# Two more pairs by seven products in the dense groups of a hybrid encoder block, with some low parts made by adding transfers

## The chip, the core and the metric

The kernel runs on one core of one Trainium2 chip. The metric is the device time of one execution in microseconds (us). TensorE (PE) multiplies, VectorE (DVE) and ScalarE (ACT) work element by element, GpSimd (POOL) here mainly issues transfers, SyncE (SP) issues nearly all loads. Each engine runs its own list of instructions in order and waits on semaphores for the others.

## The reference, cut to what matters

One encoder layer, 256 rows wide in the sequence and 4096 in the model, float32 throughout:

```python
xn = rms_norm(x, norm_in_g)
q, k, v, z_a, a_c, g_c, z_c = split(xn @ w_in)          # 4096 x 14336
y_a = rms_norm(chunked_attention(q, k, v, rel_table), attn_out_g) * silu(z_a)
y_c = rms_norm(conv_module(a_c, g_c, ...), conv_out_g) * silu(z_c)
h = x + concat([y_a, y_c]) @ w_out                       # 4096 x 4096
gate = sigmoid(rms_norm(h, ple_norm_g) @ w_ple_gate + b_ple_gate)   # 4096 x 4096
h = h + gate * (p @ w_ple)
out = rms_norm(h, final_g)
```

Nearly all work is in the products of a 256 x 4096 activation with w_in, w_out and w_ple_gate.

## The kernel before, in words

**High and low parts.** Each float32 operand is split into a high part, rounded to the format fp32r that PE multiplies, and a low part, the difference. A product of two blocks is three matmuls: high by high (kind 0), low by high (kind 1), and high by low (kind 2), where the second factor is the weight. The weights are split as they arrive (`parts_of`, L199): ACT casts the tile `wt` into `wh`, DVE subtracts it from `wt` into `wl`. `wt` has five buffers, `wh` and `wl` three each.

**Groups and pairs.** A product is made in groups of 1024 output columns (two blocks j of 512, called apart) by 256 rows (two halves h of 128). The 4096 rows of a weight are 32 blocks of 128; two of them (k0, k1) are a *pair*, so a group walks over 16 pairs. `mixed_product` (L344) makes one group in the four PSUM banks `acc`, one 128 x 512 result each, and for each pair takes one of two ways:

- A *plain* pair is the eight block products of a 2 x 2 by 2 x 2 block multiplication, 8 x 3 = 24 matmuls of 128x512.
- A pair *by sevens* (marked `*` or `+`) uses a scheme in seven products, 21 matmuls. It needs sums of the four weight blocks w00, w01 (of k0) and w10, w11 (of k1): ua = (w00 + w01, w01 + w11), then ub0 = ua1 + w11 and ub1 = ub0 + w10, all on DVE (L469, L470, L476, L477), each pair of sums split again on ACT and DVE into `uh` and `ul`. It also needs four combinations s of the activation blocks, which are made once (`combine_again`, L287: one 512-wide sum, then `combined_parts`, L261: four 128-wide operations and the split) and kept in tiles. The products are called P1 to P7 and are multiplied in the order P1, P5, P7, P2, P3, P6, P4; P1, P5, P6, P7 gather in four helper banks, which are worked into the results once a group, after its last pair by sevens (`on_helpers`, `helper_sums` L511, into the tiles z). P2 and P3 use k1's weight blocks w10 and w11. Of the activation, block (k0, second half) is not read by the seven products.

An order is a text such as `dense` (L329), which names the pairs of a group in order, with their marks. `dense` has eight pairs by sevens, all even ones; `late` (L342) has four. The combinations of the even pairs stand in tiles of their own.

**The stages.** First come groups for the convolution, queries, keys and values, in other orders, with convolution taps as filling work on DVE; the mark `+` there has the sums ua made by a transfer from GpSimd that adds to what a first transfer wrote (L423). Then `w_pw` (two groups), then the *dense groups*: four gate groups z_a and z_c (`gated`, L1064), four groups of the output projection w_out (loop at L1134, the first in order `late`, while its operands are still being made), three of the last stage (`gated_pair`, L1171, the first in order `late`) and a last group in order `final`, written out by hand.

**What sets the order.** The framework's planner places instructions: the program's text gives priorities and dependencies, and the planner, with its own costs, decides the order on each engine, which is then fixed. `later` is a queue of small pieces of work (evacuations, gating); after each pair a group takes some from it (`fill`). Tiles come from pools with a fixed number of buffers for each tag; an instruction that needs a new tile waits until a buffer of that tag is released. In the dense groups the pool `lpool` has two buffers for each tag: "stage" (the two tiles z of a group), "u", "uh" and "ul", and three for "row" (bias rows, final_g rows, scratch for combinations).

Of the kernel before, what the change touches and what calls it, by code (L numbers as in the profile page):

```python
# [16 lines left out]
P = 128  # L17
NB = 512
# [7 lines left out]
def hybrid_block(  # L26
# [184 lines left out]

    recent = []
# [48 lines left out]
    def combined_parts(dst, at, s, a, a01, a11, g, then=lambda ins: None):  # L261
# [6 lines left out]
        then(nc.vector.tensor_tensor(s3, a00, a10, ALU.subtract))  # L268
# [18 lines left out]
    def combine_again(dst, at, t, i, rows, then=lambda ins: None):  # L287

        a, s = rows
        then(  # L290
            nc.vector.tensor_tensor(
                a.rearrange("q (i t) -> q i t", t=T), t[:, i : i + 2, 0, :].bitcast(F32),
                t[:, i : i + 2, 1, :].bitcast(F32), ALU.add,
            )
        )
        return combined_parts(dst, at, s, a[:, :T], a[:, T : T + P], a[:, T + P :], 1.0, then)
# [27 lines left out]
    def units(text):  # L324

        return [(int(u.rstrip("*+")), u[-1] if u[-1] in "*+" else "") for u in text.split()]


    dense = units("1 0* 3 2* 5 4* 6* 7 8* 9 10* 11 12* 14* 13 15")  # L329
# [12 lines left out]
    late = units("1 3 5 7 9 11 13 15 0* 2 4* 6 8* 10* 12 14")  # L342

    def mixed_product(  # L344
# [14 lines left out]
        for n, (_, seven) in enumerate(order[: len(order) - n_left]):  # L359
# [45 lines left out]

        sums = {}
# [23 lines left out]
        last_seven = max((n for n, (_, seven) in enumerate(order) if seven), default=None)  # L430
        for n, (pair, seven) in enumerate(order):
# [41 lines left out]
            w1h, w1l = parts_of(w1, 2)[0]  # L473
# [7 lines left out]
            def s_of(i):  # L481
                t, at = comb[pair] if isinstance(comb, dict) else (comb[pair // 4], pair % 4)
# [576 lines left out]
    for c in range(2, D // NB):  # L1059
        if c % 2 == 0:  # L1060
            comb_tile(xS, 1)
        combine_again(xS[c // 2], 2 * (c % 2), xT[c], 0, sum_rows())()

    def gated(ys, c0, col, r_y, order, ahead):  # L1064

        _, z = sum_tiles()

        def on_helpers(helper):
            nc.scalar.copy(z[0][0], helper["P1"])
# [64 lines left out]
    for c0 in range(0, D // NB, 2):  # L1134
# [8 lines left out]
        def on_helpers(helper):  # L1143
# [9 lines left out]
            w_out[0], c0 * NB, yT, yS, dense if c0 else late, on_helpers,  # L1153
# [17 lines left out]
    def gated_pair(c0, order, ahead):  # L1171

        _, z = sum_tiles()
        rows, fgs = [], []
# [4 lines left out]
        def on_helpers(helper):  # L1179
            stt(z[0][0], helper["P1"], r_h[:, :1], rows[0], ALU.mult, ALU.add)  # L1180
# [179 lines left out]
```

## Time and profile before

| | |
|---|---|
| Median of three runs | 2029.99 us (2028.84 to 2030.45) |
| Span of the profiled execution | 2027.3 us |
| Lies around the span, against the median | 2.7 us |
| Clock granted to TensorE | full in all stages before the last |
| Busy PE, DVE, ACT, POOL | 99%, 95%, 60%, 2% |
| DMA | 436.70 MB, 215 GB/s |

The span runs from the first instruction to the last of one profiled execution; the runs are timed whole. A window's row gives its length, then busy time and number of instructions of each engine. A row of the timeline gives start, duration, engine, line, operation, tiles written and read, and in brackets how long the engine had been idle and what ended the wait.

### The profile page before, as it was taken

The page shows a single profiled execution, that of the slowest core. Times are in us where ns is not written, and L with a number is a line of the kernel's source. Part 1 is how long each engine was busy: PE and PEld are TensorE (multiplying, and loading weights), DVE is VectorE, ACT ScalarE, POOL GpSimd, SP SyncE. Part 2 cuts the span into 40 slices and gives each one's busy share as a digit, 9 for nine tenths or more (in the row PEclk, how much of TensorE's full clock was granted, in tenths as well). Part 3 has the DMA queues.
Part 4 walks back from the last instruction along what each step waited for, and adds up shares of the span by engine and source line. Part 5 has one row for each costly group of instructions (what it writes and reads, how often), then busy time and mean ns, then how long its engine had stood idle before and what let it go on. Part 6 is the DMA issues. An engine that isn't in the chain of part 4 may idle for free.

```text
span 2027.3 us, 26222 instructions
## 1 busy us (share of the span) xinstructions
PE 2010.3 (99%) x9064; PEld 1652.2 (81%) x9064; DVE 1917.8 (95%) x2732; ACT 1222.7 (60%) x1591; POOL 46.9 (2%) x50
## 2 busy tenths in 40 slices
PE   9999999999999999999999999999999999999997
PEld 7888888878888888788888888888888888888876
DVE  7999999889999998888899999999999999999998
ACT  7655545665656556776556566676665666665555
POOL 0000000000000000000000000000000000000000
PEclk9999999999999999999999999999999999999999
DMA  8787878678669867556666666676666656666765
GB/s 293 222 237 236 253 219 249 177 227 256 192 198 268 251 202 239 157 176 213 192 210 204 206 203 214 210 239 209 203 210 199 208 191 204 207 219 205 233 206 181
DMA packets 171168, 436.70 MB, mean 215 GB/s; under 512 B 13966, under 2 KB 17182, under 8 KB 171034
## 3 DMA queue, kind: packets, MB, share of 16 engines
q1 hardware_dynamic: 161952, 417.93, 64.1%
q0 software_dynamic: 8432, 16.25, 4.7%
q8 instruction: 71, 1.16, 0.3%
q10 hardware_dynamic: 650, 0.84, 0.1%
q14 instruction: 63, 0.52, 0.1%
HBM read 430.77 MB, written 4.19 MB: 215 GB/s over the span
## 4 chain that ended last, share of the span: by engine, by line
PE 92%; DVE 4%; issue 2%; DMA 1%; ACT 1%; POOLq 0%; POOL 0%; ACTq 0%; DVEq 0%
PE acc L387 71%; PE acc_P L387 17%; DVE wl L205 1%; PE tmp_ps L170 1%; DVE cv L726 1%; PE acc L229 1%; DMA wt<-in_w_in_dram 1%; DVE ul L205 1%; PE tmp_ps L898 0%; PE tmp_ps L882 0%; PE tmp_ps L916 0%; DVE cv L807 0%; PE tmp_ps L921 0%; ACT uh L204 0%; PE acc L375 0%
## 5 line engine op out<-in xcount | busy, mean ns | idle before, releaser
L387 PE MATMUL acc<-wh,big_t 128*128 128x512 f32 x4112 | 1271.6, 391 | 0.9 <-DVE y_c L1051 0.7
L204 ACT CAST wh<-wt 128x1024 fp32r<-128x1024 f32 (+1 forms) x737 | 708.8, 972 | 514.6 <-PE acc L387 359.8
L387 PEld LDWEIGHTS acc<-wh,big_t 128*128 128x128 f32 x4112 | 768.9, 188 | 160.4 <-DVE y_c L1051 1.1
L205 DVE TENSOR_TENSOR wl<-wt,wh 128x1024 fp32r<-128x1024 f32 (+1 forms) x737 | 816.7, 1120 | 33.4 <-ACT wh L204 27.8
L387 PE MATMUL acc<-wl,big_t 128*128 128x512 f32 x2056 | 794.5, 392 | 0.1
L387 PEld LDWEIGHTS acc<-wl,big_t 128*128 128x128 f32 x2056 | 385.5, 188 | 81.6 <-DVE wl L205 2.0
L204 ACT CAST uh<-ua 128x1024 fp32r<-128x1024 f32 x180 | 189.4, 1052 | 95.9 <-DVE ua L470 46.4
L205 DVE TENSOR_TENSOR ul<-ua,uh 128x1024 fp32r<-128x1024 f32 x180 | 219.5, 1220 | 5.0 <-ACT uh L204 3.2
L726 DVE SCALAR_TENSOR_TENSOR cv<-uT,dw,cv 128x255 f32<-128x255 f32 (+23 forms) x480 | 204.2, 465 | 1.1
L387 PE MATMUL acc_P<-uh,big_t 128*128 128x512 f32 x528 | 161.8, 391 | 0.1
L204 ACT CAST uh<-ub 128x1024 fp32r<-128x1024 f32 x92 | 96.8, 1052 | 92.5 <-DVE ub L477 81.1
L205 DVE TENSOR_TENSOR ul<-ub,uh 128x1024 fp32r<-128x1024 f32 x92 | 112.2, 1220 | 6.3 <-ACT uh L204 5.5
L387 PEld LDWEIGHTS acc_P<-uh,big_t 128*128 128x128 f32 x528 | 98.0, 188 | 23.0 <-ACT uh L204 3.5
L387 PE MATMUL acc_P<-ul,big_t 128*128 128x512 f32 x264 | 101.1, 391 | 0.1
L469 DVE TENSOR_TENSOR ua<-wt 128x512 f32<-128x512 f32 x105 | 72.0, 686 | 17.6 <-DMA wt<-in_w_in_dram 11.5
L387 PE MATMUL acc<-uh,big_t 128*128 128x512 f32 x272 | 84.1, 390 | 0.0
L387 PE MATMUL acc_P<-wh,big_t 128*128 128x512 f32 x272 | 84.0, 389 | 0.0
L470 DVE TENSOR_TENSOR ua<-wt 128x512 f32<-128x512 f32 x105 | 71.8, 684 | 3.2 <-DMA wt<-in_w_in_dram 3.1
L387 PE MATMUL acc_P<-uh,comb_t 128*128 128x512 f32 x228 | 70.2, 391 | 0.4 <-ACT uh L204 0.3
L477 DVE TENSOR_TENSOR ub<-ub,wt 128x512 f32<-128x512 f32 x92 | 63.1, 686 | 0.8
L476 DVE TENSOR_TENSOR ub<-ua,wt 128x512 f32<-128x512 f32 x92 | 62.9, 684 | 0.3
L387 PEld LDWEIGHTS acc<-uh,big_t 128*128 128x128 f32 x272 | 51.1, 188 | 10.6
(244 smaller groups left out, 1518.9 us busy)
## 6 DMA issues: line engine op xcount, KB each, us to landing
wt<-in_w_in_dram SPq DMA_DIRECT2D x416, 512.0 KB, 4.6
wt<-in_w_out_dram SPq DMA_DIRECT2D x128, 512.0 KB, 4.2
wt<-in_w_ple_gate_dram SPq DMA_DIRECT2D x128, 512.0 KB, 4.2
wt<-in_w_pw_dram SPq DMA_DIRECT2D x32, 512.0 KB, 4.7
ua<-in_w_in_dram SPq DMA_DIRECT2D x31, 512.0 KB, 4.5
ua<-in_w_in_dram POOLq DMA_DIRECT2D x31, 512.0 KB, 8.4
wt<-in_w_in_dram SPq DMA_DIRECT2D x31, 256.0 KB, 2.9
hc<-in_x_dram SPq DMA_DIRECT2D x8, 512.0 KB, 4.2
```

The lines of the kernel that those rows point to most:

```text
L170: nc.tensor.transpose(pt[:, i * T + h * P : i * T + (h + 1) * P], src[:, h, b] if len(src.shape) == 4 else src[:, h, b * P : (b + 1) * P], ...
L204: nc.scalar.copy(wh[:, :kc, :], wt[:, :kc, :]),
L205: nc.vector.tensor_tensor(wl[:, :kc, :], wt[:, :kc, :], wh[:, :kc, :].bitcast(F32), ALU.subtract),
L229: nc.tensor.matmul(acc, a, b[:, k, :], start=kb == 0 and kind == 0, stop=kb == kblocks - 1 and kind == 2,)
L387: nc.tensor.matmul(banks[name], a, b, start=name not in begun, stop=final and ends[name] == n and kind == 2 and not (left and name in "P2 ...
L469: plus(ua[:, 0], w0[:, 0], w0[:, 1])
L470: plus(ua[:, 1], w0[:, 1], w1[:, 1])
L476: plus(ub[:, 0], ua[:, 0], w1[:, 1])
L477: plus(ub[:, 1], ub[:, 0], w1[:, 0])
L726: nc.vector.scalar_tensor_tensor(cv[:, i, PAD - k :], uT[:, i, : T + k - PAD], dw[:, b, k : k + 1], cv[:, i, PAD - k :], ALU.mult, ALU.add,)
```

## The change

- The orders of the dense groups. `denser`, for the four gate groups and the second to fourth of the output projection, has ten pairs by sevens (the even ones, 13 and 9). `dense`, now only for the second and third group of the last stage, has nine (the even ones and 13). The order of the pairs within a group changes too. `late` and `final` stay.
- The combinations of pairs 13 and 9 are written into blocks of the activation tiles that no later product reads: block (k0, second half) of pairs 0, 2, 4, 6 for pair 13, and of pairs 8, 10, 12, 14 for pair 9. This is done once before the gates (both), once after the first group of the output projection (both), once after the first group of the last stage (13 only).
- A mark `-` in an order: five pairs of a `denser` group (2, 4, 8, 10 by sevens, 5 plain), four of a `dense` group (3, 5, 7, 9, all plain). There the low part of the weight's second block (k1) is not subtracted on DVE. ACT writes the negative of the weight, rounded, into a tile "low" (tag "stage"), and a transfer from GpSimd reads the same weights from memory again and adds them to it. The matmuls of kind 2 that use it are put off to the end of the next pair.
- Since "low" shares its tag with the tiles z, these are now allocated when the helpers are worked in, not at the group's start.

```diff
+    def high_and_minus(wt):
+        wh = wpool.tile([P, KC, NB], F32R, tag="wh", name="wh", bufs=3)
+        nc.scalar.copy(wh, wt)
+        low = spool.tile([P, KC, NB], F32R, tag="stage", name="low")
+        nc.scalar.activation(low, wt, AF.Identity, scale=-1.0)
+        return wh, low
...
         def split():
+            if at_places:
+                for i, (hi, lo) in enumerate(at_places):
+                    src = s[:, i * P : (i + 1) * P]
+                    nc.scalar.copy(hi, src)
+                    nc.vector.tensor_tensor(lo, src, hi.bitcast(F32), ALU.subtract)
+                return
...
-    dense = units("1 0* 3 2* 5 4* 6* 7 8* 9 10* 11 12* 14* 13 15")
+    dense = units("1 0* 2* 3- 4* 13* 5- 6* 8* 7- 10* 12* 9- 14* 11 15")
+    denser = units("1 0* 2*- 3 4*- 13* 5- 6* 8*- 7 10*- 12* 9* 14* 11 15")
...
+    def spare_places(tiles):
+        return [[t[:, 0, q, P:] for q in range(2)] for t in tiles]
+    places = {}
+    def combine_into_places(pair, tiles, first=0):
+        rows = sum_rows()
+        places[pair] = spare_places(tiles[first : first + 4])
+        t, i = tiles[pair // 2], pair % 2 * 2
+        combine_again(None, None, t, i, rows, at_places=places[pair])()
...
+        waiting = []
+        def add_waiting(n):
+            while waiting and waiting[0][0] <= n:
+                waiting.pop(0)[1]()
...
             if not seven:
-                for k in range(2):
-                    add_plain(n, k, *parts_of(wts[k], 2)[0])
+                add_plain(n, 0, *parts_of(wts[0], 2)[0])
+                if by_dma:
+                    wh, low = high_and_minus(wts[1])
+                    nc.gpsimd.dma_start(
+                        low, two_columns(w, 2 * pair + 1, col, apart), accum_op=ALU.add
+                    )
+                    add_plain(n, 1, wh, low, kinds=range(2))
+                    waiting.append((n + 1, partial(add_plain, n, 1, wh, low, kinds=(2,))))
+                else:
+                    add_plain(n, 1, *parts_of(wts[1], 2)[0])
+                add_waiting(n)
...
-            w1h, w1l = parts_of(w1, 2)[0]
+            if by_dma:
+                w1h, w1l = high_and_minus(w1)
+                nc.gpsimd.dma_start(
+                    w1l, two_columns(w, 2 * pair + 1, col, apart), accum_op=ALU.add
+                )
+            else:
+                w1h, w1l = parts_of(w1, 2)[0]
...
             def s_of(i):
+                if pair in places:
+                    return places[pair][i]
...
-            add("P2", block(k1, 0), (w1h[:, 0], w1l[:, 0]), n, True)
-            add("P3", s_of(3), (w1h[:, 1], w1l[:, 1]), n, True)
+            for name, x, j in (("P2", block(k1, 0), 0), ("P3", s_of(3), 1)):
+                part = partial(add, name, x, (w1h[:, j], w1l[:, j]), n, True)
+                part(kinds=range(2 if by_dma else 3))
+                if by_dma:
+                    waiting.append((n + 1, partial(part, kinds=(2,))))
...
+            add_waiting(n)
...
+    combine_into_places(13, xT)
+    combine_into_places(9, xT, 4)
...
-                ys, c0, o_z, r_y, dense,
+                ys, c0, o_z, r_y, denser,
...
-            w_out[0], c0 * NB, yT, yS, dense if c0 else late, on_helpers,
+            w_out[0], c0 * NB, yT, yS, denser if c0 else late, on_helpers,
...
+        if c0 == 0:
+            combine_into_places(13, yT)
+            combine_into_places(9, yT, 4)
...
+        if c0 == 0:
+            combine_into_places(13, hT)
```

More of the change, by code (lines that the diff above doesn't have):

```diff
@@ L259, in sum_rows, with combined_parts @@
         return [spool.tile([P, NB], F32, tag="row", name="comb", bufs=3) for _ in range(2)]
-    def combined_parts(dst, at, s, a, a01, a11, g, then=lambda ins: None):
+    def combined_parts(dst, at, s, a, a01, a11, g, then=lambda ins: None, at_places=None):
         a00, a10 = a[:, :P], a[:, P:]
@@ L285, in combine, with combine_again @@
         combined_parts(dst, at, s, a[:, :T], pts[1][:, :P], pts[1][:, P:], g[:, 1:2])()
-    def combine_again(dst, at, t, i, rows, then=lambda ins: None):
+    def combine_again(dst, at, t, i, rows, then=lambda ins: None, at_places=None):
         a, s = rows
@@ L295, in combine_again @@
         )
-        return combined_parts(dst, at, s, a[:, :T], a[:, T : T + P], a[:, T + P :], 1.0, then)
+        return combined_parts(
+            dst, at, s, a[:, :T], a[:, T : T + P], a[:, T + P :], 1.0, then, at_places
+        )
     def comb_tile(combs, n_kept=0):
@@ L324, in units @@
     def units(text):
-        return [(int(u.rstrip("*+")), u[-1] if u[-1] in "*+" else "") for u in text.split()]
-    dense = units("1 0* 3 2* 5 4* 6* 7 8* 9 10* 11 12* 14* 13 15")
+        return [
+            (int(u.rstrip("*+-")), "".join(f for f in "*+" if f in u), "-" in u)
+            for u in text.split()
+        ]
+    dense = units("1 0* 2* 3- 4* 13* 5- 6* 8* 7- 10* 12* 9- 14* 11 15")
+    denser = units("1 0* 2*- 3 4*- 13* 5- 6* 8*- 7 10*- 12* 9* 14* 11 15")
     first = units("0 1 3 5 7 9 11 13 15 2* 8 4* 10 6* 12 14")
@@ L358, in mixed_product @@
         n_left = len(left) // 2
-        for n, (_, seven) in enumerate(order[: len(order) - n_left]):
+        for n, (_, seven, _) in enumerate(order[: len(order) - n_left]):
             for name in ("P1", "P5", "P6", "P7", "P2", "P3", "P4") if seven else ("P2", "P3", "P4", "X"):
@@ L429, in mixed_product @@
                 after.enter_context(tc.issue_after(ins.ins))
-        last_seven = max((n for n, (_, seven) in enumerate(order) if seven), default=None)
-        for n, (pair, seven) in enumerate(order):
+        last_seven = max((n for n, (_, seven, _) in enumerate(order) if seven), default=None)
+        for n, (pair, seven, by_dma) in enumerate(order):
             if n < done:
@@ L1171, in gated_pair @@
     def gated_pair(c0, order, ahead):
-        _, z = sum_tiles()
-        rows, fgs = [], []
+        z, rows, fgs = [], [], []
         def on_begin():
@@ L1179, in on_helpers @@
         def on_helpers(helper):
+            z.extend(sum_tiles()[1])
             stt(z[0][0], helper["P1"], r_h[:, :1], rows[0], ALU.mult, ALU.add)
```

4 lines of the change are left out of this document (3 added, 1 removed).

## The prediction, made before the result was known

> **What bounds the kernel now.** I read the page first, then the chain of waits in order of time, then busy time by stretch, cut where the evacuation of each group of products begins.
>
> ```profile
> span 2027.3 us, 26222 instructions
> ...
> PE 2010.3 (99%) x9064; PEld 1652.2 (81%) x9064; DVE 1917.8 (95%) x2732; ACT 1222.7 (60%) x1591; POOL 46.9 (2%) x50
> ...
> PE 92%; DVE 4%; issue 2%; DMA 1%; ACT 1%; POOLq 0%; POOL 0%; ACTq 0%; DVEq 0%
> ...
> 1138.99 11.56 PE acc L387 x51
> ```
>
> The last row gives the price of one 128x512 matmul: 11.56 / 51 = 0.2267 us. The mean of 391 ns in other views is the latency of overlapping ones. TensorE sets the end, but VectorE is only 4 points behind, so the question is asked per group:
>
> ```profile
> 940.70:984.80 44.10, 44.10 (x195) 36.35 (x195) 35.75 (x56) 25.14 (x33) 0.00 (x0) 1.00 0.60 190
> ...
> 984.80:1067.90 83.10, 82.43 (x364) 67.89 (x363) 77.04 (x93) 50.58 (x59) 0.69 (x1) 1.00 0.64 203
> 1067.90:1149.70 81.80, 81.58 (x360) 67.25 (x359) 78.14 (x93) 49.15 (x54) 0.00 (x0) 1.00 0.64 205
> 1149.70:1231.10 81.40, 81.38 (x359) 67.10 (x358) 78.25 (x94) 49.02 (x54) 0.00 (x0) 1.00 0.65 207
> 1231.10:1314.00 82.90, 82.90 (x375) 68.88 (x375) 78.20 (x98) 50.33 (x61) 0.00 (x0) 1.00 0.66 214
> 1314.00:1404.40 90.40, 90.40 (x422) 74.78 (x422) 87.41 (x140) 59.24 (x85) 0.00 (x0) 1.00 0.68 223
> 1404.40:1485.60 81.20, 81.20 (x360) 67.21 (x359) 78.00 (x93) 48.53 (x57) 0.00 (x0) 1.00 0.63 207
> 1485.60:1567.70 82.10, 81.99 (x362) 67.58 (x361) 78.26 (x94) 48.94 (x59) 0.00 (x0) 1.00 0.63 205
> 1567.70:1651.20 83.50, 83.50 (x378) 69.34 (x377) 80.19 (x101) 52.12 (x67) 0.00 (x0) 1.00 0.64 208
> 1651.20:1741.50 90.30, 90.30 (x425) 75.18 (x424) 85.03 (x136) 59.12 (x91) 0.69 (x1) 1.00 0.62 197
> 1741.50:1829.10 87.60, 87.55 (x384) 71.35 (x383) 86.95 (x107) 53.48 (x64) 0.00 (x0) 1.00 0.66 212
> 1829.10:1917.20 88.10, 88.10 (x386) 71.76 (x385) 87.24 (x107) 52.40 (x64) 0.00 (x0) 1.00 0.67 216
> ```
>
> After the length come PE, PEld, DVE, ACT and POOL, then clock, DMA share and GB/s. The changed groups are rows 2 to 5 (gates), 7 to 9 (output projection) and 11 and 12 (last stage). A dense group is 360 matmuls, 360 x 0.2267 = 81.6 us: PE runs at its pace. But DVE is busy 78 of it, and 87 in the last stage. That leaves some 3.5 us a group before DVE becomes the bound.
>
> **The change, part by part.**
>
> *Matmuls.* A plain pair is 8 block products of 3 matmuls, a pair by sevens 7 of 3. Two more sevens in seven groups and one more in two: (7 x 2 + 2) x 3 = 48 matmuls fewer, 10.9 us if nothing else moved: 1.36 in each of the seven groups, 0.68 in the two.
>
> *VectorE.* Its prices are from start to start, since neighbours overlap:
>
> ```profile
> 1144.92 1.05 ACT L204 CAST wh<-wt 128x1024 fp32r<-128x1024 f32 x1 [1.67 <-PE acc L387]
> 1145.53 0.69 DVE L470 TENSOR_TENSOR ua<-wt 128x512 f32<-128x512 f32 x1 [0.33 <-DMA wt<-in_w_in_dram]
> 1146.14 0.68 DVE L476 TENSOR_TENSOR ub<-ua,wt 128x512 f32<-128x512 f32 x1
> 1146.86 0.69 DVE L477 TENSOR_TENSOR ub<-ub,wt 128x512 f32<-128x512 f32 x1
> 1147.46 1.22 DVE L205 TENSOR_TENSOR wl<-wt,wh 128x1024 fp32r<-128x1024 f32 x1
> 1148.60 1.22 DVE L205 TENSOR_TENSOR ul<-ua,uh 128x1024 fp32r<-128x1024 f32 x1
> 1149.73 2.48 DVE L1075 TENSOR_TENSOR z<-acc,z 128x512 f32<-128x512 f32 x4
> ...
> 1153.26 1.41 DVE L184 SCALAR_TENSOR_TENSOR qT<-qT,r_a,z 128x512 f32<-128x512 f32 x2
> 1153.44 1.04 ACT L204 CAST wh<-wt 128x1024 fp32r<-128x1024 f32 x1
> ```
>
> A 512-wide operation is 0.60 (0.72 between the two for ub, the second of which needs the first), a 1024-wide one 1.14. A plain pair is two low parts, 2.28. A pair by sevens is one 512-wide low part, four sums and three 1024-wide low parts: 0.60 + 0.60 + 0.60 + 0.72 + 0.60 + 3 x 1.14 = 6.54. So a pair moved costs DVE 4.26, and a low part made by a transfer gives back 1.14. The seven groups: 2 x 4.26 - 5 x 1.14 = +2.82. The last stage: 4.26 - 4 x 1.14 = -0.30. DVE then needs 78.14 + 2.82 = 80.96 in the second gate group, where PE needs 354 x 0.2267 = 80.25. **The bound changes engine**, and the saving is cut by the difference.
>
> *DVE's idle time.* No queue of dependent work runs quite without gaps. In the two last-stage groups, where DVE is nearly full now, it idles 87.60 - 86.95 = 0.65 and 88.10 - 87.24 = 0.86. The nearest rows on the other side:
>
> ```profile
> 183.10:268.60 85.50, 85.50 (x383) 70.80 (x382) 85.50 (x141) 44.25 (x49) 5.17 (x5) 1.00 0.81 240
> ...
> 445.90:531.70 85.80, 85.80 (x384) 71.00 (x383) 85.13 (x139) 47.01 (x53) 6.39 (x6) 1.00 0.89 254
> ```
>
> In the first DVE idles 0.00, but there convolution taps without a deadline fill each gap; dense groups have none. The upper bound is the 3.4 to 3.6 of today's gate groups. I take 0.75, by the rows nearest in kind and in load.
>
> *Combinations.* Five calls; each makes on DVE one 512-wide sum, four 128-wide operations and four 128-wide low parts, and four 128-wide copies on ACT.
>
> ```profile
> L291 DVE TENSOR_TENSOR comb<-big_t 128x512 f32<-128x512 f32 x16 | 11.0, 688 | 0.1
> ...
> L268 DVE TENSOR_TENSOR comb<-comb 128x128 f32<-128x128 f32 x31 | 8.9, 287 | 0.9 <-ACT comb L284 0.7
> ```
>
> With no overlap 0.69 + 8 x 0.287 = 2.99; with the 0.08 overlap of the rows above, 0.60 + 8 x 0.20 = 2.2; I take 2.6. The two for the gates (5.2) fall where DVE idles 44.10 - 35.75 = 8.35, mostly waiting for ACT: nothing, up to 5.2 if they are put off into the first gate group. The two of the output projection come after its first group, which has 90.40 - 87.41 - 0.75 = 2.24 to spare; 2.96 is left for the next one. The one of the last stage needs two "row" buffers of three, and two of these hold final_g until products put off into the next group are done, so its 2.6 falls there. DVE ends each first group on two plain pairs, with its buffers full, and part of the excess can be paid from that lead: between all and none, I take half, 1.48 and 1.30.
>
> *Low parts by transfer.* Each puts on ACT one more pass of about 1.05 (same size as the cast), and a pair by sevens casts three and a half tiles where a plain pair casts two, so ACT rises from 49 to 49 + 5 x 1.05 + 2 x 1.6 = 57.5 of 81, under PE. The negative may have to wait for one of the two "stage" buffers, and all later casts queue behind it on ACT, and DVE's low parts behind those. In the gates both hold the gate's sums until the products at L184: the first is free at 1153.26 + 1.41 = 1154.7, 5.4 us into a group that starts at 1149.3, and the first negative (pair 2, after pairs 1 and 0) is wanted some 8 us in, so no wait; in the last stage three pairs go by first. POOL, empty in those groups, issues five transfers.
>
> ```profile
> L423 POOLq EVENT_SEMAPHORE  x31: 17/43/43, 89.3 to 786.6; - x31
> L423 POOL DMA_DIRECT2D ua<-in_w_in_dram x31: 1213/1222/1359, 89.9 to 787.2; - x31
> DMA to landing us min/median/max: 6.1/8.4/10.4
> ...
> q0 software_dynamic: 8432, 16.25, 4.7%
> ```
>
> These 31 are adding transfers of the same 512 KB. One takes 4.7% x 2027 / 31 = 3.1 us of all DMA engines; five lift the share from 0.64 to 0.64 + 15.4 / 81.8 = 0.83, below the 0.89 under which PE and DVE are both full above. Weights should not come late. The low part lands 0.6 + 8.4 = 9.0 us after ACT made the negative. The matmuls that need it are put off to the end of the next pair: from P2 on, 10 + 21 matmuls (7.0 us) when the next pair is by sevens. For 4 and 10, which follow plain pairs, the cast's buffer comes free 21 matmuls (4.76) before P2, so the negative is ready at best 4.76 - 2.1 = 2.66 before it: 9.7 in all, 0.7 to spare. The cast at 1153.44 is such a one. It ends 2.5 us before its P2 (33 matmuls into that group, about 1157.0), which leaves 1.5 for the negative, 8.5 in all: 0.5 late. The other three have 11.3 or more. I cost this at nothing, since a PE wait of 0.5 twice is under the 81.7 - 80.25 = 1.45 by which DVE is longer; beyond that it counts.
>
> The Trainium skill, "DMA: Bandwidth & Descriptors", section "Anatomy of one DMA", fits a GpSimd-issued transfer as 2.0 us plus bytes over 436 GB/s, which would be an estimated 3.2 us for this size; the adding transfers measured here take 8.4, and the measurement decides. By the page's fit the late low parts below would not exist, and the sum would be the same.
>
> **The sum**, per group the longer of DVE (busy + change + 0.75) and PE, less the length now:
> gates: 83.10 - 1.36 = 81.74 by PE, -1.36; 81.71, -0.09; 81.82, +0.42; 81.77, -1.13.
> Output projection: 81.57 + 1.48 = 83.05, +1.85; 81.83, -0.27; 83.76, +0.26.
> Last stage: 86.95 - 0.30 + 0.75 + 1.30 = 88.70, +1.10; 87.69, -0.41.
> Together +0.4 us. The profiled execution's span is 2027.3 and the median of the runs 2029.99; the 2.7 between them lies around the span. 2027.3 + 0.4 + 2.7 = **2030.4 us**: no change that can be measured (0.2%, 4.1 us, is about the least that can be told).
>
> **Rivals.**
> *A, DVE runs nearly without gaps.* For it: 85.50 of 85.50 above. Against: dense groups have no filler. With no idle time and all combinations under cover, the nine groups give -1.36, -0.84, -0.33, -1.36, -0.38, -1.02, -0.49, -0.68, -0.68 = -7.1, so 2022.9; with 0.25 idle in six of them, 2024.4. Faster.
> *B, the low parts come late.* Place: the deferred matmuls of pairs 4 and 10. At 9.5 us to landing, inside the range above, the first waits 0.6 + 9.5 - 8.5 = 1.6; ACT then gets ahead by that, up to its buffers' 9.7, and the second waits 0.4. PE is 80.25 + 2.0 = 82.25, 0.5 above DVE's 81.75; if ACT does not get ahead, 83.45, 1.7 above. Seven groups: +3.5 to +12; I take +6, nearer the end at which ACT's buffers fill: 2036. It decides once the waits of a group pass 1.45. Slower.
> *C, bursts.* Pairs 12, 9 and 14 in a row need 3 x 6.54 of DVE against 3 x 4.76 of PE. Each needs its 6.54 by its 18th matmul (3.85 us), so DVE must come in 2.7 + 2 x 1.78 = 6.3 us ahead, and two or three buffers hold about 7. Where it is not, PE waits, and DVE idles later at full buffers: 1.5 instead of 0.75 idle in seven groups, +5: 2036. Slower.
>
> **How the numbers follow.** My forecast 0.40, A 0.27, B 0.22, C 0.11. So faster 0.27, same 0.40, slower 0.33. The range runs from A's full gain, 2023, to B with much of its upper price, 2040. The forecast's own range is 2026 to 2034.
>
> **What will show it.** Steps right: 48 matmuls fewer; DVE 80.5 to 81.5 busy in gate groups two and three, group length 81.2 to 82.3; DVE, not PE, named in the chain of waits in these groups; the group after each first group longer by 1 to 2 us. A: these groups under 81.2. B: PE waiting on the DMA into "low", some 1 us a time, twice a group. C: PE waiting on ul or wl in pairs 9 and 14. I am wrong if DVE in a gate group is busy under 80 us, or if the combinations cost more than 3 us each.

## The result: 2.4% slower, with waiting where the prediction had none

| | median us | runs |
|---|---|---|
| before | 2029.41 | 2028.75 to 2030.45 |
| changed | 2079.38 | 2076.58 to 2081.64 |
| ratio | 1.0243 | 95% interval 1.0229 to 1.0258 |

The forecast was 2030.4, its range 2023 to 2040. The change costs 50 us, and 49 of them were not in the sum. The head of the page after, its GpSimd queue (the 31 transfers of the early stages and the 43 new ones) and the shares of the chain:

```profile
span 2074.7 us, 26434 instructions
...
PE 2020.5 (97%) x9016; PEld 1639.3 (79%) x9016; DVE 1947.2 (94%) x2830; ACT 1289.6 (62%) x1686; POOL 84.7 (4%) x93
...
q0 software_dynamic: 14624, 38.80, 11.1%
...
PE 74%; DVE 11%; DMA 6%; issue 4%; ACT 3%; ACTq 0%; SPq 0%; POOLq 0%; POOL 0%; DVEq 0%
```

The matmuls fell by 48, as counted. But no engine took over as the bound: PE, DVE and ACT all have a smaller or hardly larger share of a longer span, and the chain, 92% PE before, now passes through DVE, DMA and ACT. The same view by stretch as before, cut at the same evacuations (length, PE, PEld, DVE, ACT, POOL, clock, DMA share, GB/s):

```profile
983.70:1069.60 85.90, 82.98 (x355) 66.98 (x354) 79.97 (x103) 56.97 (x69) 5.40 (x6) 0.98 0.78 226
1069.60:1157.00 87.40, 82.79 (x356) 65.41 (x355) 79.64 (x99) 56.32 (x63) 4.33 (x5) 1.00 0.76 218
1157.00:1245.20 88.20, 83.16 (x356) 65.49 (x355) 81.02 (x100) 56.54 (x64) 4.33 (x5) 1.00 0.76 220
1245.20:1335.20 90.00, 85.42 (x374) 67.35 (x373) 83.28 (x109) 59.64 (x72) 4.36 (x5) 1.00 0.77 228
1335.20:1427.90 92.70, 90.97 (x423) 74.81 (x423) 90.11 (x149) 60.31 (x90) 0.00 (x0) 1.00 0.66 219
1427.90:1511.80 83.90, 81.60 (x351) 64.60 (x350) 80.86 (x105) 56.23 (x68) 4.33 (x5) 1.00 0.76 233
1511.80:1597.30 85.50, 82.28 (x355) 65.68 (x355) 80.95 (x100) 56.36 (x67) 4.32 (x5) 1.00 0.75 227
1597.30:1685.80 88.50, 84.89 (x371) 68.79 (x370) 82.78 (x104) 58.10 (x72) 4.34 (x5) 0.98 0.73 221
1685.80:1780.20 94.40, 92.71 (x431) 76.00 (x431) 89.78 (x143) 60.60 (x95) 0.71 (x1) 1.00 0.62 198
1780.20:1872.50 92.30, 87.41 (x378) 69.68 (x377) 87.31 (x116) 59.93 (x74) 3.53 (x4) 1.00 0.73 225
1872.50:1964.70 92.20, 88.62 (x382) 70.81 (x381) 87.31 (x109) 57.93 (x70) 3.48 (x4) 1.00 0.74 228
```

These eleven rows add up to 981.0, against 932.4 before: all of the loss is here. In the second row DVE was to be busy 80.96 and is busy 79.64, so its work was sized well (99 instructions, where 93 + 7 were to be), but it idles 7.8 us instead of 0.75, while PE idles 4.6. (PE's busy time itself hides more: 356 matmuls at 0.2267 are 80.7, and gaps shorter than a matmul's 0.39 of latency don't show.) When both idle in one group, they wait in turn for a third party. The chain of waits of this one group, by line, before and after:

```profile
by line: PE acc L387 72.6%; PE acc_P L387 26.6%; DVE ul L205 1.4%; DVE z L1075 0.7%; issue 0.2%
```

```profile
by line: PE acc L420 25.4%; DMA wt<-in_w_in_dram 16.9%; PE acc_P L420 14.0%; issue 9.4%; DVE wl L205 8.8%; DVE ul L205 7.9%; ACT uh L204 5.8%; DVE ua L518 2.7%; DVE ua L519 2.2%; DVE ub L531 2.1%; DVE ub L532 1.8%; DVE qT L184 1.2%; ACT wh 
```

The third party is the loads of the weights: 16.9% of the group hangs on them, 0% before. Who stands and waits for them is in the waits of the single engines (in total, times, longest), first over the dense groups before, then after:

```profile
DVE ul L205 <- ACT uh L204: 5.4, 7, 1.2
...
PE acc L387 <- DVE y_c L1051: 0.7, 1, 0.7
```

```profile
ACT low L217 <- DMA wt<-in_w_in_dram: 30.0, 14, 4.6
...
ACT low L217 <- DMA wt<-in_w_out_dram: 14.5, 8, 4.6
...
DVE ul L205 <- ACT uh L204: 30.8, 26, 3.1
...
PE acc_P L420 <- ACT uh L204: 25.9, 26, 2.7
```

It is ACT, at the negative for "low" (the last stage adds 4.0 in 2 times, 48.5 in 24 in all). DVE and PE then wait for `uh`, the cast of a weight sum, which has nothing to do with "low". One such place in the timeline, ACT first, then one row of DVE and two of PE:

```profile
1094.69 1.04 ACT L204 CAST wh<-wt 128x1024 fp32r<-128x1024 f32 x1
1098.36 1.06 ACT L217 ACTIVATE low<-wt 128x1024 fp32r<-128x1024 f32 x1 [2.62 <-DMA wt<-in_w_in_dram]
1099.33 1.03 ACT L204 CAST wh<-wt 128x1024 fp32r<-128x1024 f32 x1
1100.26 1.04 ACT L204 CAST uh<-ua 128x1024 fp32r<-128x1024 f32 x1
1101.20 1.04 ACT L215 CAST wh<-wt 128x1024 fp32r<-128x1024 f32 x1
...
1096.88 0.68 DVE L519 TENSOR_TENSOR ua<-wt 128x512 f32<-128x512 f32 x1
...
1098.23 0.84 PE L420 MATMUL acc<-wh,big_t 128*128 128x512 f32 x3
1101.35 1.19 PE L420 MATMUL acc_P<-uh,big_t 128*128 128x512 f32 x4 [2.28 <-ACT uh L204]
```

L217 is the negative, L215 the cast of the same tile. The text has the cast first; the planner has put the negative 2.84 us ahead of it, and ahead of two casts (L204) that belong to other tiles. One is `uh`, whose sum ua DVE has ready at 1096.88 + 0.68 = 1097.56. ACT stands at the negative until the load lands, 2.62 us, then serves the others, and `uh` starts 2.7 us after it could have; PE loses 2.28. So two suspects stand in one row: the place in ACT's order, and a load that is late. From issue to landing the weight loads (nearly all of them of w_in) took, in the window 985 to 1330 (min, median, max in us), before and after:

```profile
DMA to landing us min/median/max: 3.4/4.1/6.9
```

```profile
DMA to landing us min/median/max: 3.4/4.7/7.6
```

The median hides how many are late. Counted load by load in the two traces, over all rows of the table, 51 of 312 weight loads take more than 6 us after the change, 3 of 313 before. ACT waits 63.5 us for weight loads in these rows (48.5 at the negatives, the rest at casts), and 51.5 of it is spent on loads that took more than 5 us. So the loads that ACT stands for are mostly slow after their issue, and not only issued late.

### The profile page after: what moved, and what is told of

Read it like the earlier page. It is cut to its first block, busy times and chain, and to the rows that moved or that the text cites. A ratio compares the mean times of both kernels' runs of the same rounds, so it can differ in the third digit from the quotient of the medians.

```text
span 2074.7 us, 26434 instructions
## 1 busy us (share of the span) xinstructions
PE 2020.5 (97%) x9016; PEld 1639.3 (79%) x9016; DVE 1947.2 (94%) x2830; ACT 1289.6 (62%) x1686; POOL 84.7 (4%) x93
## 3 DMA queue, kind: packets, MB, share of 16 engines
q0 software_dynamic: 14624, 38.80, 11.1%
## 4 chain that ended last, share of the span: by engine, by line
PE 74%; DVE 11%; DMA 6%; issue 4%; ACT 3%; ACTq 0%; SPq 0%; POOLq 0%; POOL 0%; DVEq 0%
PE acc L420 57%; PE acc_P L420 13%; DVE wl L205 3%; DMA wt<-in_w_in_dram 3%; DMA wt<-in_w_out_dram 2%; DVE ul L205 2%; ACT uh L204 2%; ACT wh L204 1%; PE tmp_ps L170 1%; DMA wt<-in_w_ple_gate_dram 1%; PE acc L237 1%; DVE ua L518 1%; DVE ua L519 1%; DVE cv L787 1%; DVE ub L531 1%
## 5 line engine op out<-in xcount | busy, mean ns | idle before, releaser
L420 PE MATMUL acc<-wh,big_t 128*128 128x512 f32 x3920 | 1205.0, 392 | 4.0 <-ACT wh L204 2.4
L204 ACT CAST wh<-wt 128x1024 fp32r<-128x1024 f32 (+1 forms) x694 | 658.3, 956 | 466.6 <-PE acc L420 325.8
L420 PEld LDWEIGHTS acc<-wh,big_t 128*128 128x128 f32 x3920 | 733.7, 188 | 157.8 <-ACT wh L204 3.2
L205 DVE TENSOR_TENSOR wl<-wt,wh 128x1024 fp32r<-128x1024 f32 (+1 forms) x694 | 761.5, 1106 | 34.7 <-ACT wh L204 29.9
L420 PE MATMUL acc<-wl,big_t 128*128 128x512 f32 x1848 | 709.8, 393 | 2.1 <-DVE wl L205 1.9
L420 PEld LDWEIGHTS acc<-wl,big_t 128*128 128x128 f32 x1848 | 346.1, 188 | 78.6 <-DVE wl L205 7.4
L204 ACT CAST uh<-ua 128x1024 fp32r<-128x1024 f32 x196 | 205.6, 1049 | 101.5 <-DVE ua L519 53.8
L420 PE MATMUL acc_P<-uh,big_t 128*128 128x512 f32 x624 | 191.0, 396 | 24.1 <-ACT uh L204 24.1
L204 ACT CAST uh<-ub 128x1024 fp32r<-128x1024 f32 x108 | 113.2, 1048 | 39.1 <-DVE ub L532 36.8
L518 DVE TENSOR_TENSOR ua<-wt 128x512 f32<-128x512 f32 x121 | 83.0, 686 | 4.3 <-DMA wt<-in_w_in_dram 3.4
L519 DVE TENSOR_TENSOR ua<-wt 128x512 f32<-128x512 f32 x121 | 83.0, 686 | 0.9 <-DMA wt<-in_w_in_dram 0.7
L420 PEld LDWEIGHTS acc_P<-ul,big_t 128*128 128x128 f32 x312 | 58.5, 189 | 22.1 <-DVE ul L205 9.7
L217 ACT ACTIVATE low<-wt 128x1024 fp32r<-128x1024 f32 x43 | 45.5, 1058 | 48.5 <-DMA wt<-in_w_in_dram 30.0
```

The lines of the kernel that those rows point to most:

```text
L204: nc.scalar.copy(wh[:, :kc, :], wt[:, :kc, :]),
L205: nc.vector.tensor_tensor(wl[:, :kc, :], wt[:, :kc, :], wh[:, :kc, :].bitcast(F32), ALU.subtract),
L217: nc.scalar.activation(low, wt, AF.Identity, scale=-1.0)
L420: nc.tensor.matmul(banks[name], a, b, start=name not in begun, stop=final and ends[name] == n and kind == 2 and not (left and name in "P2 ...
L518: plus(ua[:, 0], w0[:, 0], w0[:, 1])
L519: plus(ua[:, 1], w0[:, 1], w1[:, 1])
```

## The experiments

All medians stand against the kernel before on the same chip (2029.1 to 2029.7). e1 to e4 separate the parts, e5 to e8 test the place and the transfers alone, e9 to e14 the bytes, the margin and a smaller dose.

**e1: the negative behind its cast.** In `high_and_minus`:

```diff
-        nc.scalar.copy(wh, wt)
+        cast = nc.scalar.copy(wh, wt)
-        nc.scalar.activation(low, wt, AF.Identity, scale=-1.0)
+        with tc.issue_after(cast.ins):
+            nc.scalar.activation(low, wt, AF.Identity, scale=-1.0)
```

> One edit to the changed kernel: on ScalarE the negative of the weight ("low") is queued behind the high-part cast of the same weight instead of where the planner put it (ahead of it, as soon as the planner thought the weight had landed). Theory 1, the place on ScalarE: 29 or so waits of the negative on weight loads, 48 us in sum, mostly vanish (under 10 us), the gate groups go from 86 to 90 us down to 81.5 to 83, and the whole to 2028 to 2042. Theory 2, DMA load (the adding transfers delay the weights themselves, wherever the negative stands): the waits move to the casts and the time stays within 8 us of 2079. Theory 3, VectorE as the bound (my forecast): no change from 2079 either, since VectorE's work is the same.

Measured 2054.67, ratio 1.0130 (1.0114 to 1.0147), between the ranges of theories 1 and 2: half of the loss goes with one constraint on order. PE's waits for `uh` fall from 25.9 to 5.9 us. But the planner answers the constraint with further moves: about 230 of DVE's 2830 instructions, all in the dense groups, stand in another place of its order too. So this is a comparison of two orders, which differ in more than the 43 negatives. What is left is partly the late low part of rival B, which the changed kernel itself never showed (PE's waits in the dense groups of e1):

```profile
PE acc L421 <- DMA low<-in_w_out_dram: 5.9, 4, 2.1
PE acc_P L421 <- ACT uh L204: 5.9, 10, 1.1
PE acc L421 <- DMA low<-in_w_in_dram: 3.3, 5, 1.2
```

**e2: all low parts on DVE again**, the ten and nine pairs by sevens kept.

```diff
-    dense = units("1 0* 2* 3- 4* 13* 5- 6* 8* 7- 10* 12* 9- 14* 11 15")
-    denser = units("1 0* 2*- 3 4*- 13* 5- 6* 8*- 7 10*- 12* 9* 14* 11 15")
+    dense = units("1 0* 2* 3 4* 13* 5 6* 8* 7 10* 12* 9 14* 11 15")
+    denser = units("1 0* 2* 3 4* 13* 5 6* 8* 7 10* 12* 9* 14* 11 15")
```

> The changed kernel with the marks for adding transfers taken out of both orders: ten and nine pairs by seven products, all low parts on VectorE. VectorE then needs about 79.6 + 5 x 1.14 = 85.3 to 86.7 us in a gate group and 91 in the last stage. All theories have VectorE as the bound here: gate groups 86 to 88 us with VectorE busy over 98% of them, ScalarE never waiting on a weight load for a negative, 2070 to 2085 in all. Theory 2 alone also says that weight loads in the gates land in 4.2 us on average again instead of 5.0. If it is faster than 2060, my prices of VectorE are wrong.

Measured 2079.07, 1.0247 (1.0231 to 1.0262): the same time as the change, for another reason. The second gate group:

```profile
1070.80:1157.70 86.90, 83.49 (x355) 64.97 (x354) 86.45 (x104) 52.48 (x59) 0.00 (x0) 1.00 0.63 194
```

DVE is busy 86.45 of 86.90. The prediction's prices give 80.96 + 5 x 1.14 = 86.66, and the idle time is 0.45, so DVE's prices hold, and a DVE that really is the bound idles as little as was assumed. Without the transfers the weight loads land in 3.3, 3.8 and 6.3 us (min, median, max, window 985 to 1330).

**e3: the transfers alone.** Eight pairs by sevens as before, four adding transfers a group, no new combinations.

```diff
+    dense = units("1 0* 3- 2* 5- 4* 6* 7- 8* 9- 10* 11 12* 14* 13 15")
+    denser = units("1 0* 3- 2* 5- 4* 6* 7- 8* 9- 10* 11 12* 14* 13 15")
...
-    combine_into_places(...)        # all five
```

> The kernel before with its own order of pairs (eight by seven products) and no extra combinations, but four plain pairs of each dense group (3, 5, 7, 9) make their second low part by an adding transfer, with the negative placed by the planner. VectorE gets 4.6 us a group lighter, TensorE's work is unchanged. Theory 1: ScalarE stands at the negatives waiting for loads and the nine groups lose 1 to 5 us each: 2038 to 2070. Theory 2: the same range, from the weights' own lateness (loads 0.5 to 1 us longer). Theory 3: nothing is lost, 2026 to 2032.

Measured 2081.36, 1.0259 (1.0241 to 1.0278), above every range that was stated. The transfers alone, which take work off DVE, add a pass on ACT and leave PE's work as it was, cost 52 us. ACT waits 52.7 us at the negatives for loads in the dense groups, and DVE 68.7 us at ua.

**e4: the combinations alone**: both orders as `dense` was before, the five combinations still made, unused.

```diff
+    dense = units("1 0* 3 2* 5 4* 6* 7 8* 9 10* 11 12* 14* 13 15")
+    denser = units("1 0* 3 2* 5 4* 6* 7 8* 9 10* 11 12* 14* 13 15")
```

> The changed kernel with both dense orders set back to those of before, so that the five combinations into unread blocks are made but not used, with no adding transfers for low parts. My forecast's prices: 13 us of VectorE work, of which 2 to 8 us show: 2031 to 2037, in the gate's first group and in the groups around the first ones of the output projection and of the last stage. Theories 1 and 2 say the same. If it takes over 2045, the combinations are a main cause.

Measured 2031.61, 1.0011 (1.0002 to 1.0020): 2.3 us, with the later allocation of the tiles z in it. The sum had 1.48 + 1.30 = 2.8.

**e5: the negative made from the cast**, which forces the same place by a dependency.

```diff
-        nc.scalar.activation(low, wt, AF.Identity, scale=-1.0)
+        nc.scalar.activation(low, wh.bitcast(F32), AF.Identity, scale=-1.0)
```

> One edit to the changed kernel: the negative is made from the high part already cast instead of from the weight tile (the same values), so that it cannot stand ahead of the cast and releases the weight's buffer earlier. Theory 1 (place on ScalarE): like the run with the negative behind its cast, 2048 to 2056, a little less if buffers come free sooner. Theory 2 (DMA load): 2075 to 2083.

Measured 2053.05, 1.0118 (1.0103 to 1.0133), as e1: the same place, forced in two ways, gives the same time. Low is the weight less the rounded weight either way.

**e6: e1 with the late matmuls put off by two pairs** in `denser`.

```diff
+        put_off = 2 if order is denser else 1
-                    waiting.append((n + 1, partial(part, kinds=(2,))))
+                    waiting.append((n + put_off, partial(part, kinds=(2,))))
```

> The run with the negative behind its cast, and the matmuls that use the transferred low parts put off by two pairs instead of one in the seven denser groups. Rival B of the prediction (low parts late): the 11 us of TensorE waits on the transfers into low vanish from the gates and the output projection, 2040 to 2047. If the waits only move to ScalarE's and VectorE's products, 2050 to 2056.

Measured 2054.98, 1.0125 (1.0110 to 1.0140): nothing gained. PE's waits for "low" fall from 9.9 us to 0.7, and those for `uh` rise from 5.9 to 12.1. The waits moved; so rival B was a symptom in e1, not the cause of its 25 us.

**e7: e3 with the negative behind its cast** (the edits of e3 and e1 together).

```diff
+        with tc.issue_after(cast.ins):
+            nc.scalar.activation(low, wt, AF.Identity, scale=-1.0)
...
+    denser = units("1 0* 3- 2* 5- 4* 6* 7- 8* 9- 10* 11 12* 14* 13 15")
```

> Transfers alone (order of pairs and combinations as before, four low parts a group by transfer), with the negative queued behind its cast. Theory 1: nearly all of the 52 us lost by the transfers alone comes back, 2028 to 2040, since TensorE's work is that of before and VectorE's is 4.6 us a group less. Theory 2 (the DMA load itself): 2060 to 2085.

Measured 2091.17, 1.0303 (1.0287 to 1.0319): worse than e3, and above the range of theory 2 too. That the place of the negative is the whole matter falls with this run. The waits of DVE in the dense groups, and under them PE's:

```profile
DVE ua L519 <- DMA wt<-in_w_in_dram: 31.8, 15, 5.2
DVE ua L519 <- DMA wt<-in_w_out_dram: 27.5, 14, 4.2
...
PE acc L421 <- DVE wl L205: 39.0, 19, 4.0
```

One such place in the timeline of DVE:

```profile
1042.76 0.69 DVE L519 TENSOR_TENSOR ua<-wt 128x512 f32<-128x512 f32 x1 [5.15 <-DMA wt<-in_w_in_dram]
1043.95 0.69 DVE L520 TENSOR_TENSOR ua<-wt 128x512 f32<-128x512 f32 x1 [0.50 <-DMA wt<-in_w_in_dram]
1044.56 1.22 DVE L205 TENSOR_TENSOR wl<-wt,wh 128x1024 fp32r<-128x1024 f32 x1
```

It is the same pattern on another engine: the sum ua of a coming pair stands in front of the low part `wl` that PE needs next, and waits 5.15 us for a load. Before, this wait came to 7.8 us for w_in over all dense groups (8 times, 1.7 at most). In all, the 52.7 us of ACT at the negatives are gone against e3, and DVE's waits at ua for loads rise from 68.7 to 106.4. In both orders the instruction that stands first after a load takes the wait, with all that is behind it.

**e8: adding transfers that nobody reads.** Orders as in e3, but DVE makes all low parts, and the transfers (36) go into a zeroed scratch tile.

```diff
...
-                    wh, low = high_and_minus(wts[1])
+                    unused = spool.tile([P, KC, NB], F32, tag="stage", name="unused")
+                    nc.gpsimd.memset(unused, 0.0)
                     nc.gpsimd.dma_start(
-                        low, two_columns(w, 2 * pair + 1, col, apart), accum_op=ALU.add
+                        unused, two_columns(w, 2 * pair + 1, col, apart), accum_op=ALU.add
                     )
...
+                add_plain(n, 1, *parts_of(wts[1], 2)[0])
```

> The kernel before with the same number of adding transfers from GpSimd, at the same pairs, into a scratch tile that nothing reads (zeroed by GpSimd first); all low parts are subtracted on VectorE as before and ScalarE makes no negatives. What is left of the change is only the load on the DMA engines. Theory 2: weight loads land about 0.6 us later and the time rises to 2050 or more. Theory 1: loads land later too, but the buffers cover it: 2028 to 2036.

Measured 2052.07, 1.0116 (1.0099 to 1.0132): 22.4 us from transfers whose result nobody reads. PE, DVE and ACT run the instructions of the kernel before, in its order, and only GpSimd ever waits for the scratch tile, though it shares its tag with z. GpSimd's 36 zeroings (0.96 us each) are new too, but DVE is no slower beside them: a 1024-wide low part takes 1218 ns in both. DVE's waits of ua for loads grow to 12.0 + 11.5 + 7.3 + 1.5 = 32.3 us, from 7.8 + 4.3 + 1.6 = 13.7 before: 18.6 more, and the profiled execution is 2046.7 - 2027.3 = 19.4 longer. The waits of DVE:

```profile
DVE ua L516 <- DMA wt<-in_w_in_dram: 12.0, 12, 3.0
DVE ua L516 <- DMA wt<-in_w_out_dram: 11.5, 7, 3.3
DVE ua L517 <- DMA wt<-in_w_in_dram: 7.3, 4, 3.7
```

The weight loads from issue to landing in the window of above, the longest 11.7 us instead of 6.9:

```profile
DMA to landing us min/median/max: 3.4/4.4/11.7
```

**e9 and e10: the changed kernel and e1 with an eighth of the bytes.** Each transfer adds only the first 128 of 1024 columns, 64 KB instead of 512; the rest of these low parts is never completed, so most of what they give is missing from the results. The order of the instructions on PE, DVE, ACT and GpSimd is that of the changed kernel, and of e1.

```diff
+        def add_some(low, kb):
+            nc.gpsimd.dma_start(
+                low[:, 0, :P], w[kb * P : (kb + 1) * P, col : col + P], accum_op=ALU.add
+            )
-                    nc.gpsimd.dma_start(
-                        low, two_columns(w, 2 * pair + 1, col, apart), accum_op=ALU.add
-                    )
+                    add_some(low, 2 * pair + 1)
...
```

> The changed kernel with every adding transfer into low cut from 512 to 64 KB (128 of 1024 columns), so that most of these low parts are left out of the result; the order of instructions on every engine is unchanged. Theory 1 alone (the negative's place on ScalarE costs, whatever the DMA does): ScalarE still stands for weights and it takes 2060 or more. Theory 2 (the bytes of the adding transfers make weight loads late, and the fixed orders turn that into stalls): 2024 to 2040, with weight loads landing in 4.2 us on average.

> The kernel with the negative behind its cast, with the same cut of the transfers to 64 KB (most of these low parts left out), the order on every engine unchanged. Theory 2: the 25 us that were left go to under 6: 2024 to 2035, near the sum of the prediction (2030). If 15 us or more stay, something else than the DMA load, such as VectorE or the combinations, holds them.

Measured 2045.88, 1.0085 (1.0070 to 1.0100), and 2040.89, 1.0059 (1.0044 to 1.0074). Both lie 6 us above theory 2's range. With instructions and order unchanged, the bytes alone are 33.5 us of the changed kernel. The weight loads of e9 in the window 985 to 1330:

```profile
DMA to landing us min/median/max: 3.3/4.3/6.3
```

Over all dense rows 3 of 313 take more than 6 us, against 51 of 312 with the full transfers. The negatives still wait for their loads, 32.6 us in all, but 2.7 at most instead of 4.6, and PE's waits for `uh` fall from 25.9 to 7.2 us: the shorter waits are mostly covered, the longer ones are not. In e10 the second to fourth gate group and the row behind them are:

```profile
1065.20:1146.40 81.20, 81.20 (x354) 65.55 (x353) 79.44 (x98) 56.14 (x63) 4.33 (x5) 1.00 0.68 206
1146.40:1229.00 82.60, 82.32 (x357) 66.08 (x357) 80.62 (x101) 56.11 (x64) 4.33 (x5) 1.00 0.68 208
1229.00:1315.30 86.30, 85.92 (x385) 69.15 (x385) 84.61 (x116) 61.57 (x77) 4.36 (x5) 1.00 0.69 210
1315.30:1406.50 91.20, 89.65 (x411) 73.11 (x410) 88.11 (x143) 57.45 (x85) 0.00 (x0) 1.00 0.68 223
```

The first two rows have about the lengths that the prediction gave, but not its bound. The chain of waits of the first one passes through PE alone:

```profile
by line: PE acc L421 65.5%; PE acc_P L421 34.9%
```

**e11: e8 with plain transfers** instead of adding ones.

```diff
-                        unused, two_columns(w, 2 * pair + 1, col, apart), accum_op=ALU.add
+                        unused, two_columns(w, 2 * pair + 1, col, apart)
```

> The kernel before with unused transfers of 512 KB from GpSimd as in the run before, but plain copies instead of adding ones. The bytes read from memory are the same. If the adding (3.1 us of all DMA engines each, against 1.6 for a plain load) is what delays the weights, the loss falls from 22 us to 5 to 12: 2034 to 2042; if the bytes read are, it stays at 2048 to 2055.

Measured 2039.20, 1.0051 (1.0036 to 1.0066): 10.1 us, so a little over half of e8's 22.4 belongs to the adding. The order is that of e8 on every engine, so the two can be compared matmul by matmul. By the end of the gates (1314 us before) e8 is 9.1 us late and e11 0.3; by the last stage (1741.5) 16.6 and 2.2; at the end of its dense groups (1917.2) 19.4 and 10.8. So in the gates only the adding costs, and most of what the plain transfers cost comes in the last stage. In the window 985 to 1330 the twelve adding transfers hold 9.8% of the DMA engines' time, the twelve plain ones 5.3%, and the longest load is 7.7 us instead of 11.7.

**e12: the kernel before with one weight buffer fewer** (`wt`, four instead of five, in all stages).

```diff
-    wpool = pool("wpool", 5)
+    wpool = pool("wpool", 4)
```

> The kernel before with four weight buffers instead of five, so that each load is issued about 2.5 us later against its use. It measures how much lateness the loads can bear. Theory 2 needs a small margin: 2050 or more. If it stays under 2035, loads have more than 2.5 us to spare and lateness of 1 to 3 us cannot be the cause.

Measured 2043.46, 1.0067 (1.0050 to 1.0084): 14.4 us, between the two bounds. The kernel before cannot give a buffer away for nothing. But with four buffers the planner makes another order as well (about a quarter of DVE's 2732 instructions stand in another place, and PE's order differs), so the 14.4 us are not the price of the lead alone. More buffers were not tried.

**e13: e3 with an eighth of the bytes** (the edit of e9 on e3).

```diff
...
+                    add_some(low, 2 * pair + 1)
```

> Transfers alone (the order of pairs and the combinations of before, four low parts a group by transfer, the negative where the planner put it), with each transfer cut from 512 to 64 KB, so that most of these low parts are left out of the result; the order on TensorE, VectorE, ScalarE and SyncE is unchanged against the run with full transfers (2081). If the bytes make the loss, it goes to 2027 to 2040; if the planned order by itself does, it stays over 2060.

Measured 2038.22, 1.0043 (1.0027 to 1.0060): with e3's order unchanged on every engine, 43 of its 52 us are bytes.

**e14: a smaller dose.** Nine pairs by sevens and two transfers a group in the seven groups, the last stage as before, combinations for pair 13 only, the negative behind its cast.

```diff
+    dense = units("1 0* 3 2* 5 4* 6* 7 8* 9 10* 11 12* 14* 13 15")
+    denser = units("1 0* 2* 3- 4* 13* 5 6* 8* 7- 10* 12* 9 14* 11 15")
...
-    combine_into_places(9, ...)     # and those of the last stage
```

> A smaller dose, complete result: in the gates and in the second to fourth group of the output projection nine pairs by seven products (the even ones and 13) and two low parts by transfer (pairs 3 and 7) with the negative behind its cast; the last stage as before. VectorE 78.2 + 4.26 - 2.28 = 80.2 busy with 1.8 idle as in the run with small transfers, TensorE 357 x 0.2267 = 80.9: about 82 a group against 81.8 now, plus 0.5 to 1.5 a group for the load of two transfers: 2030 to 2042. If it comes under 2025, a smaller dose of the change would have been worth it.

Measured 2031.22, 1.0011 (1.0001 to 1.0020): no gain. None of the runs beats the kernel before.

## Why the prediction was wrong, point by point

**The step that failed** is "Low parts by transfer", and in it the sentence that a DMA share of 0.83 lies "below the 0.89 under which PE and DVE are both full" and that "weights should not come late". The share came out lower still (0.76 to 0.78 in the gates), and the weights came late. The share of busy DMA time did not tell here how long a load takes, nor whether anybody stands for it. In the row at 0.89 (445.9 to 531.7 of the kernel before) the weight loads take as long as in the changed kernel, and no engine waits for one:

```profile
DMA to landing us min/median/max: 3.7/5.0/8.1
```

That stage has another order, in which taps fill DVE's gaps; which of its differences lets it bear such loads is open. What the runs put in the place of the sentence is a table of two causes, each taken away with the other kept:

| negative | 512 KB | 64 KB |
|---|---|---|
| where the planner put it | 2079.4 | 2045.9 |
| behind its cast | 2054.7 | 2040.9 |

With small transfers the bad place costs 5.0 us, with full ones 24.7; with the good place the bytes cost 13.8, with the bad one 33.5. Each row compares bytes with the order unchanged. Each column compares two orders, which differ in more than the place (e1). The causes do not simply add. The reading that fits is that late loads hurt where the order lets an instruction that depends on them stand in front of older work. Of the miss of 49.0, taken in the order bytes, place, rest, 33.5 + 5.0 + 10.5; place first would make it 24.7 + 13.8 + 10.5. Why one adding transfer makes other loads late is not shown.

The Trainium skill, "DMA: Bandwidth & Descriptors", section "Queues, rings and completion order", says that each DMA engine takes turns between the queues that have work for it. The longer loads of SP's queue beside GpSimd's transfers agree (median 4.1 to 4.7 us here); the runs don't show the turns themselves.

**The place of the negative** was costed at nothing as well, on the ground that it had no wait for a "stage" buffer. That was so. But the wait for the weight itself was not looked for, though the prediction named what queues behind the negative. 48.5 us of ACT's idle time is this wait; ACT's total of 57.5 of 81 was right (56.3) and of no use, since ACT is late at one place, not too slow.

**"The bound changes engine"** failed too. In the changed kernel no engine is the bound of the gates. In e10, with both causes small, the first three gate groups take 245.3 us, as forecast (245.3), and the second and third of the output projection 163.8 against 164.9; but the chains of the first two gate groups are PE alone, while DVE idles 1.8 us in the second, and in the other groups PE has the larger part of the chain. The forecast's length for the second came from DVE's 80.96 + 0.75, so the agreement is luck. In the gates DVE was the bound only where it kept all low parts (e2).

**The rest, 10.5 us.** In e10 the eleven rows add up to 945.1, the forecast's to 932.8. The excess lies where stages change: the fourth gate group with the next row 177.5 against 81.8 + 90.4, +5.3; the fourth of the output projection with the next row 178.6 against 83.8 + 90.3, +4.5; and the last two, 179.9 against 176.4, +3.5. At the first of these DVE is busy 84.61 + 88.11 = 172.7, 7.1 more than before where 2.82 was forecast, with 21 more instructions where a denser group has 7 more: most of the output projection's combinations (9 instructions each) fell into rows that the sum took as unchanged. By the tiles they write, 12 of their 18 stand in these two rows and 6 in the next. No run isolates what they cost beside the denser orders.

**Right**: the 48 matmuls; DVE's prices (e2); combinations (2.3 us measured, 2.8 in the sum); the landing of "low", 8.4 taken, 7.4 in the median (5.4 to 9.5); 3.1 us of all DMA engines for one adding transfer (11.1% x 2074.7 / 74 = 3.1). DVE's idle 0.75 holds where DVE is the bound (e2: 0.45); in e10 it is 1.8 to 2.0, with 79.44 busy where 80.96 was forecast.

**The rivals.** A (no idle time) fell. B named the right resource, a transfer that is late, and the wrong victim: in the changed kernel PE never waits for "low", and its waits of 9.9 us in e1 only moved when they were taken away (e6). C: PE's waits for ul and wl are 2.2 and 1.9 us in all, no burst. The sign "wrong if DVE is busy under 80" did go off (79.64), but by chance: it was to catch wrong prices, and the prices held. The thing to name was DVE's idle time.

## What to carry to other kernels

Before adding transfers to a stage whose engines run in a fixed order, find each instruction that stands first after a load and ask what is queued behind it; where there is no lead to spare, a few slower loads become stalls on every engine. The busy share of DMA did not tell this here, and bytes that nobody reads, sent beside the kernel before in an unchanged order, measure it directly. Taking a buffer away measures the lead only if the order stays, so compare the orders first. Where a new instruction and an old one wait for the same load, tie the new one behind the old one: here the order that came of it was worth 25 us, though in another order (e7) the wait only went to the next engine.

## What the hardware showed beyond that

An adding transfer takes nearly twice the DMA time of a plain one of the same 512 KB (9.8% against 5.3% of the same 345 us, for twelve) and disturbs the loads beside it more: the longest takes 11.7 us against 7.7. And a stall can be followed by a second price. Three stretches of 3.4 us of the changed kernel, in a row:

```profile
1012.00:1015.40 3.40, 1.61 (x8) 1.01 (x7) 2.45 (x3) 3.26 (x4) 0.86 (x1) 1.00 0.81 177
1015.40:1018.80 3.40, 3.40 (x10) 2.64 (x9) 1.81 (x4) 1.51 (x2) 0.00 (x0) 0.51 0.95 235
1018.80:1022.20 3.40, 3.40 (x16) 2.82 (x15) 3.37 (x5) 1.20 (x3) 0.00 (x0) 0.99 0.92 357
```

After a stretch with 1.61 us of matmuls in 3.40, the granted clock is 0.51 for 3.4 us, and 10 matmuls start instead of 16: by estimate some 1.4 us more (6 x 0.2267), for a stall of 1.79. The Trainium skill, "TensorE: Matmul & The Clock Gate", section "Part 1: The HAM clock gate", has a gate that watches windows of about 3.4 us and halves the clock after an idle one; the trace agrees in length and factor, though the window, as cut here, was only about half idle. It happens twice in the dense groups of the changed kernel and not in those before; the mean granted clock of e7, the slowest run, is 0.991 against 0.998 in e10.
